# Operand tile of all products laid out by k-tiles with both halves side by side and 32 bytes behind each

## The chip, the cores and the metric

The kernel runs on one core of one Trainium2 chip. The metric is the device time of one execution in microseconds. Three runs of the kernel before gave 1229.66 us as their median (1229.54 to 1230.91 us).

## The reference

Two layers of a decoder trunk work on x of 256 tokens by 2048 channels, all in float32. The first layer is a Mamba-2 mixer: one wide input product, a causal convolution, a scan over one chunk of 256 tokens, a gated norm in 8 groups, and an output product. Its result makes one shared K and V. The second layer is an attention with three groups of heads on that K and V, with a gate and an output product. Every layer ends in a LayerNorm of the residual.

```
h = x * (1 + scale) + shift                 # per layer, from c
proj = h @ a_in_w                           # 2048 -> 10304
y = ssd(conv(xBC), dt) * silu(z), normed    # 256 x 4096
x = LayerNorm(ALPHA*x + (1+gate) * (y @ a_out_w))       # 4096 -> 2048
k, v = split(x @ kv_w)                      # 2048 -> 6144
h = x * (1 + scale1) + shift1
q, z = split(h @ b_in_w)                    # 2048 -> 4096
o = attention(q, k, v) * silu(z)
out = LayerNorm(ALPHA*x + (1+gate1) * (o @ b_out_w))
```

## The kernel before

Nearly all the time goes into the products with the large weights. Every float32 operand of them is split in two float32r tiles, a high half and a low half that holds what the high one lost, and a product is three matmuls: high by high, high by low, low by high. A weight piece of 128x1024 floats is loaded into a tile `raw` (6 buffers, SP's queue), ScalarE copies it to `whi` (line 100) and VectorE writes `raw - whi` to `wlo` (line 102). The other operand, with its 2048 or 4096 channels in k-tiles of 128, stays in one tile, `actT`, that the program takes four times over: as `hp` (the input of layer one, lines 339 and 340), `yp` (the input of the first output product, lines 866 and 867), `xp` (the input of K, V, the queries and the second gate, lines 944 and 945), and at the end as `gl`, which holds rows of gate and norm (line 1218) and feeds no product.

Three helpers write all these matmuls, and they use `actT` in three ways:

- `cm_piece` (lines 151 to 153): weights stationary, 256 columns of `actT` moving, four blocks of 128 output channels for each k-tile, so 12 matmuls of 256 columns for a k-tile.
- `cm_wide` (lines 190 and 193): weights stationary; for the high weights both halves of a k-tile move in one matmul of 512 columns, for the low weights the high half moves alone (256 columns). A k-tile has two of 512, then two of 256. It makes the channels `xs` of groups 2 to 7 from `hp`, and K, the queries and the second gate from `xp`.
- `tm_mults` (lines 224 to 226): the other way round. A block of 128 tokens of `actT` is stationary and 512 columns of weights move; a k-tile has six matmuls. It makes z from `hp`, the first output product from `yp`, V from `xp`, and the second output product from other tiles.

Each matmul has its own weight load, which the profile lists as PEld. The product of `dt` (lines 626 to 628) is of the first kind with 256 moving columns.

Where the bytes lie in a partition matters for what follows. `actT` begins at byte 88320, which is a multiple of 256. The k-tiles of one half of `hp` and of `yp` are 1024 bytes apart and the two halves 16 KB apart; in `xp` a k-tile has its two halves side by side and k-tiles are 2048 bytes apart. `whi` and `wlo` have four buffers each of 4352 bytes, 17 times 256, that begin at multiples of 256 too. `halves_at` shifts what is written in them by an offset that depends on the helper: `SHORT` (16 floats, 64 bytes) for `cm_piece`, `WIDE` (48 floats, 192 bytes) for `cm_wide`, `LONG` (none) for `tm_mults`. So with all distances taken modulo 256 bytes, the weights lie 64 bytes behind the operand in every matmul of `cm_piece`, 192 behind it in every one of `cm_wide`, and at the same place in every one of `tm_mults`, whatever the k-tile and the buffer.

The order of the work is that of the code: each engine runs what the program issues for it in that order, with a few `issue_after` that hold a step behind another.

Of the kernel before, what the change touches and what calls it, by code (L numbers as in the profile page):

```python
# [9 lines left out]
F32 = mybir.dt.float32  # L10
F32R = mybir.dt.float32r
# [7 lines left out]
P = 128  # L19
L = 256  # L20
D = 2048
KT = D // P
# [18 lines left out]
    _o += _s  # L41
NPAR = _o

CI, CT, CM, NCONST = 0, 128, 256, 384

CD, CG, NBIAS = 0, 512, 1024

# [2 lines left out]
def trunk(ctx, tc, xT, x, c, par, cst, bias, lnrow, ada, wdt, win, wxs, wout, wk, wv, wbin, wbout, out):  # L50
# [5 lines left out]
    act = ctx.enter_context(tc.tile_pool(name="act", bufs=1))  # L56
# [15 lines left out]
    cc = cons.tile([P, NCONST], F32, name="cc")  # L72
# [4 lines left out]

    ident = cc[:, CI:CI + 128]
    tri = cc[:, CT:CT + 128]
    ones = cc[:, CM:CM + 128]  # L80
    cons.tile([P, 32], F32, name="pad")
    SHORT, WIDE, LONG = (16, 16), (48, 48), (0, 0)

# [24 lines left out]
    def settle():  # L108

        while owed:  # L110
            with tc.issue_after(copied[-1].ins), tc.issue_after(latest[-1].ins):
                owed.pop(0)()

    def first_or(src, q, off=(0, 0)):

        return ready.pop() if ready else split(load_piece(src[q]), off=off)

    def begin_next():

        if upcoming:  # L120
            src, q, off = upcoming.pop(0)
            ready.append(split(load_piece(src[q]), off=off))

    def behind_next():

        stack = ExitStack()
        if ready:
            stack.enter_context(tc.issue_after(copied[-1].ins))
            stack.enter_context(tc.issue_after(latest[-1].ins))
        return stack  # L130

    def background(n, every=1):

        state[0] += n
        while state[0] >= every and jobs:
            state[0] -= every
            jobs.pop(0)()
# [25 lines left out]
    def acc_pair(pool=None):  # L163
        return [(pool or mm).tile([P, 2, L], F32, name="acc") for _ in range(2)]
# [10 lines left out]

    def cm_wide(src, dst, rate=(0, 1), moving=None, later=False, seen=lambda a: a):

        both, high = moving or (lambda kt: xp[:, kt], lambda kt: xhi[:, kt, :])
        ps = acc_pair()
        for q in range(KT // 4):  # L180
            w = first_or(src, q, WIDE)
            if q == 1:
                settle()
            if q == KT // 4 - 1:
                begin_next()
            hi, lo = (t.rearrange("p k n -> p (k n)").rearrange("p (k n) -> p k n", k=4) for t in w)
            for k in range(4):
                kt = 4 * q + k
                for n in range(2):
                    T.matmul(ps[n], hi[:, k, n * P:n * P + P], both(kt), start=kt == 0, stop=False,  # L190
                             skip_group_check=True)
                for n in range(2):
                    T.matmul(ps[n][:, 0, :], lo[:, k, n * P:n * P + P], high(kt), start=False, stop=kt == KT - 1,  # L193
                             skip_group_check=True)
            background(*rate)
        def put():
            for n in range(2):
                d = dst[:, n, :]
                if seen is by_time:
                    d = d.rearrange("p (b m h) -> p b m h", b=2, h=2)  # L200
                S.activation(d, seen(ps[n][:, 1, :]), AF.Copy)
                V.tensor_tensor(d, seen(ps[n][:, 0, :]), d, op=ALU.add)

        if later:
            owed.append(put)
        else:
            with behind_next():
                put()
# [127 lines left out]
            jobs.pop(0)()  # L336


    hp = act.tile([P, 2, KT, L], F32R, name="actT")
    hhi, hlo = hp[:, 0], hp[:, 1]  # L340


    slots = ctx.enter_context(tc.tile_pool(name="slots", bufs=1))
# [1 line left out]
    with ExitStack() as cA:  # L345
# [15 lines left out]
        with ExitStack() as cS:  # L361
# [38 lines left out]
            def xs_wide(g):  # L400

                xs[g] = pxs.tile([P, 4, L], F32, name="xs")
                for w in range(2):
                    t = xs[g][:, 2 * w:2 * w + 2, :]
                    cm_wide(wxs[2 * g - 4 + w], t, rate=R, moving=(lambda kt: hp[:, :, kt, :], hh_))
                    for n in range(2):
                        conv(t[:, n, :], 4 * g + 2 * w + n, t[:, n, :])

# [31 lines left out]
            with ExitStack() as c0:  # L440
# [83 lines left out]
                for row in ("b4:0. b6:0. h z2:0. z1:0. b2:0 x1:0 h", "b2:1. x1:1. z1:1. z4:0 h h",  # L524
# [3 lines left out]
                    for w in row.split():  # L528
                        if w == two:
                            n = -2 if sum(o[0] == -2 for o in order) == sum(o[0] == -1 for o in order) else -1  # L530
# [160 lines left out]
            R = (1, 10)  # L691
# [171 lines left out]
        aux = ctx.enter_context(tc.tile_pool(name="auxb", bufs=2, space=PSUM, reuse_waits="tile"))  # L863

        pn = cA.enter_context(tc.tile_pool(name="pn", bufs=1, reuse_waits="tile"))
        yp = act.tile([P, 2, KT, L], F32R, name="actT")
        yhi = [yp[:, 0], yp[:, 1]]
        ylo = {g: pn.tile([P, 4, L], F32R, name=f"ylo{g}") for g in (1, 2, 3, 4, 7, 5, 6)}

        def y_ahead(q):  # L870
# [70 lines left out]
                    normalise(b, 256, 512)  # L941


    xp = act.tile([P, KT, 2, L], F32R, name="actT")
    xhi, xlo = xp[:, :, 0, :], xp[:, :, 1, :]
    pb = ctx.enter_context(tc.tile_pool(name="pb", bufs=1))
    hx, lx = (lambda kt: xhi[:, kt, :]), (lambda kt: xlo[:, kt, :])

# [52 lines left out]
    with ExitStack() as cL:  # L1001
# [3 lines left out]
        def high(i, b):  # L1005
            for k in range(2):
                kt = 2 * (i // 2) + k
                for w in first_v[i]:
                    T.matmul(vps[i % 2][b], hx(kt)[:, b * P:b * P + P], w[:, k, :], start=kt == 0 and w is first_v[i][0],  # L1009
                             stop=False)  # L1010
# [6 lines left out]
        end, _ = x_quad(0)  # L1017
# [5 lines left out]
        for i in range(4):  # L1023
            if i == 2:
                _, tile4 = x_quad(1)
# [10 lines left out]
        for q in range(2, KT // 2):  # L1036
# [3 lines left out]
            for j in range(2):  # L1040
                with tc.issue_after(end.ins):
                    w = split(load_piece(wv[2 * j][q]), after=tile4.ins if q == 2 else None)
# [4 lines left out]
        R = (1, 2)  # L1047
# [19 lines left out]
        for kt in range(KT):  # L1067
            t = pl.tile([P, L], F32, name="htmp")
# [10 lines left out]
    R = (0, 1)  # L1079
# [135 lines left out]
        z_gate(hq, qs[hq])  # L1215
    drain()

    gl = act.tile([P, 2, 2, D], F32, name="actT")
    gt, lnt = gl[:, 0], gl[:, 1]
    og = (lambda kt: oghi[kt // 4][:, kt % 4, :]), (lambda kt: oglo[kt // 4][:, kt % 4, :])  # L1220

# [64 lines left out]
    mv0, r0, _ = root(0, lambda mv: None)  # L1286
# [29 lines left out]
    _, r1, step = root(1, between)  # L1316
# [34 lines left out]
def _layout(x, c, ada_w, ada_b, ln_g, ln_b, a_in_w, a_conv_w, a_conv_b, a_dt_bias,  # L1351
            a_A_log, a_D, a_norm_g, a_out_w, kv_w, b_in_w, b_out_w):
    f = np.float32
    crow = np.concatenate([c.reshape(KT, P), np.eye(KT, dtype=f)], 1)
    par = np.zeros((P, NPAR), f)

    def put(name, a):
        par[:a.shape[0], OFF[name][0]:OFF[name][1]] = a

    ab = ada_b.reshape(2, 3, KT, P)  # L1360
    put("adab", ab.transpose(3, 0, 2, 1).reshape(P, 96))
    put("convw", a_conv_w[0].T.reshape(48, P, 4).transpose(1, 0, 2).reshape(P, 192))
    put("convb", _cm(a_conv_b[0]))
    put("normg", _cm(a_norm_g[0]))
    put("dsk", np.broadcast_to(a_D[0], (P, 64)))
    put("dtb", a_dt_bias[0][:, None])
    put("alog", np.broadcast_to(a_A_log[0], (P, 64)))
    put("lng", _cm(ln_g[0]))
    put("lnb", _cm(ln_b[0]))

    cst = np.zeros((P, NCONST), f)
    i = np.arange(P)
    cst[:, CI:CI + 128] = np.eye(P)
    up = (i[:, None] <= i[None, :]).astype(f)
    cst[:, CT:CT + 128] = up
    cst[:, CM:CM + 128] = 1.0
    bias = np.zeros((P, NBIAS), f)
    half, m = i // 64, i % 64
    same = 4 * (m[:, None] - m[None, :]) + 2 * (half[:, None] - half[None, :])
    own = 4 * (m[:, None] - m[None, :])  # L1380
    second = half[:, None] != half[None, :]

    def mask(delta, win_, dil):
        return np.where((delta >= 0) & (delta % dil == 0) & (delta <= win_), 0.0, NEG)

    ratio = np.where(second, SLOPES[2 * H], SLOPES[H]) / SLOPES[0]
    bias[:, CD:CD + 512] = np.concatenate([-same - 1, -same, -own * ratio, 1 - same], 1)
    bias[:, CG:CG + 512] = np.concatenate([mask(same + 1, 128, 1), mask(same, 128, 1),
                                           np.where(second, mask(own, 2048, 16), mask(own, 512, 4)),
                                           mask(same - 1, 128, 1)], 1)  # L1390

    ada = ada_w.reshape(2, D, 3, KT, P).transpose(0, 2, 3, 4, 1)

    w = a_in_w[0]
    z, xs, bb, cc, dt = (w[:, a:b] for a, b in ((0, 4096), (4096, 8192), (8192, 9216), (9216, 10240), (10240, 10304)))
    bc = np.stack([bb.reshape(D, G, P), cc.reshape(D, G, P)], 2).reshape(D, 2048)
    win = _pieces(np.concatenate([bc, xs[:, :1024], z], 1))
    return {
        "xT": x[0].T.reshape(KT, P, L).transpose(1, 0, 2), "x": x[0], "c": np.concatenate([crow, np.zeros_like(crow), crow]), "par": par, "cst": cst, "bias": bias,
        "lnrow": np.stack([ln_g[0], ln_b[0], ln_g[1], ln_b[1]]),  # L1400
        "ada": ada, "wdt": _dt(dt), "win": win, "wxs": _pieces(xs[:, 1024:], 256, 4),
        "wout": _pieces(a_out_w[0]), "wk": _pieces(kv_w[:, :3072], 256, 4),
        "wv": _pieces(kv_w[:, 3072:]), "wbin": _pieces(b_in_w[0], 256, 4), "wbout": _pieces(b_out_w[0]),
    }
# [20 lines left out]
```

## Time and profile before

| | |
|---|---|
| median of 3 runs | 1229.66 us |
| the profiled execution | 1229.02 us |
| its span | 1227.2 us |
| PE busy | 1212.2 us |
| VectorE busy | 1018.8 us |
| ScalarE busy | 705.4 us |
| HBM traffic | 273 GB/s mean over the span |
| granted TensorE clock | 1.0 |

The profile is of one execution. PE is TensorE's matmuls and PEld its weight loads; DVE is VectorE, ACT is ScalarE. The matmuls overlap each other in the records: the duration of one is longer than the distance to the next one's start, so the pace of a stream is read from the starts, in the timeline, and not from the durations. The timeline merges equal instructions that follow each other into one row with their count.

### The profile page before, as it was taken

To read this page: it belongs to the slowest core of one execution; us is meant where nothing else is said; L and a number is where in the kernel's file an instruction comes from. 1 tells how busy PE (TensorE), PEld (TensorE's weight loads), DVE (VectorE), ACT (ScalarE), POOL (GpSimd) and SP (SyncE) were. 2 spreads that over 40 slices of the span, in tenths; PEclk is the share of its full clock that TensorE was granted. 3 is DMA by queue.
4 is the path that set the end of the run, shared out by engine and by line. 5 is a ranking of instruction groups with operands and counts; after the bars stand their busy time and mean duration, and the time that the engine had idled before them with its cause. 6 is when DMAs were issued, how large, how long until landed. Compare 5 with 4: busy or idle time off the path is not lost.

```text
span 1227.2 us, 19063 instructions
## 1 busy us (share of the span) xinstructions
PE 1212.2 (99%) x7244; PEld 1038.8 (85%) x7244; DVE 1018.8 (83%) x1448; ACT 705.4 (57%) x1058; POOL 3.9 (0%) x8
## 2 busy tenths in 40 slices
PE   8899999999999999999999999999999999999998
PEld 7789988898888888888888788888887888888886
DVE  6999996999988989899778578888987875756786
ACT  3555577878597789754335455444435744444751
POOL 0000000000000000000000000000000000000001
PEclk9999999999999999999999999999999999999999
DMA  9999977686666556599988669989997775365673
GB/s 372 422 421 422 422 269 243 224 304 242 226 207 205 170 168 213 188 343 337 382 298 309 217 190 350 346 343 382 383 380 277 262 275 173 112 191 162 193 258 69
DMA packets 81372, 335.94 MB, mean 274 GB/s; under 512 B 9200, under 2 KB 9984, under 8 KB 68480
## 3 DMA queue, kind: packets, MB, share of 16 engines
q1 hardware_dynamic: 80352, 333.33, 74.6%
q0 software_dynamic: 576, 1.05, 0.6%
q8 instruction: 57, 0.93, 0.3%
q10 hardware_dynamic: 352, 0.34, 0.1%
q14 instruction: 35, 0.29, 0.1%
HBM read 331.45 MB, written 3.23 MB: 273 GB/s over the span
## 4 chain that ended last, share of the span: by engine, by line
PE 81%; DMA 8%; DVE 6%; ACT 3%; issue 2%; DVEq 0%; ACTq 0%; SPq 0%
PE acc L190 24%; PE acc L193 12%; PE acc L225 11%; PE acc L226 11%; PE acc L224 11%; DMA raw<-in_win 6%; DVE wlo L102 2%; DVE araw L306 2%; PE py L787 1%; ACT whi L100 1%; PE acc L151 1%; PE acc L153 1%; DMA araw<-in_ada 1%; PE acc L152 1%; PE acc L1009 1%
## 5 line engine op out<-in xcount | busy, mean ns | idle before, releaser
L100 ACT ACTIVATE whi<-raw 128x1024 fp32r<-128x1024 f32 x389 | 408.0, 1057 | 355.8 <-PE acc L226 126.0
L102 DVE TENSOR_TENSOR wlo<-raw,whi 128x1024 fp32r<-128x1024 f32 x389 | 468.9, 1221 | 140.2 <-ACT whi L100 138.7
L190 PE MATMUL acc<-actT,whi 128*128 128x512 f32 x1280 | 401.1, 394 | 0.0
L193 PEld LDWEIGHTS acc<-actT,wlo 128*128 128x128 f32 x1280 | 239.5, 188 | 52.6 <-DVE wlo L102 0.3
L225 PE MATMUL acc<-wlo,actT 128*128 128x512 f32 x656 | 257.5, 392 | 3.3 <-DVE wlo L102 3.3
L193 PE MATMUL acc<-actT,wlo 128*128 128x256 f32 x1280 | 254.7, 280 | 0.0
L224 PE MATMUL acc<-whi,actT 128*128 128x512 f32 x656 | 253.6, 394 | 0.2 <-ACT whi L100 0.2
L306 DVE SCALAR_TENSOR_TENSOR araw<-araw,cb__72 128x2048 f32<-128x2048 f32 x95 | 217.0, 2284 | 3.4 <-DMA araw<-in_ada 3.1
L190 PEld LDWEIGHTS acc<-actT,whi 128*128 128x128 f32 x1280 | 194.7, 188 | 0.8
L226 PE MATMUL acc<-whi,actT 128*128 128x512 f32 x432 | 168.8, 391 | 0.0
L225 PEld LDWEIGHTS acc<-wlo,actT 128*128 128x128 f32 x656 | 123.2, 188 | 31.0 <-DVE wlo L102 6.0
L224 PEld LDWEIGHTS acc<-whi,actT 128*128 128x128 f32 x656 | 122.5, 188 | 24.7 <-ACT whi L100 0.6
L151 PE MATMUL acc<-actT,whi 128*128 128x256 f32 x372 | 103.0, 281 | 2.5 <-ACT s L646 1.4
L153 PE MATMUL acc<-actT,wlo 128*128 128x256 f32 x372 | 101.8, 282 | 1.4 <-DVE wlo L102 1.1
L152 PE MATMUL acc<-actT,whi 128*128 128x256 f32 x372 | 102.9, 279 | 0.0
L226 PEld LDWEIGHTS acc<-whi,actT 128*128 128x128 f32 x432 | 81.1, 188 | 16.7
L226 PE MATMUL acc<-whi,ylo 128*128 128x512 f32 x224 | 87.6, 391 | 0.0
L151 PEld LDWEIGHTS acc<-actT,whi 128*128 128x128 f32 x372 | 69.7, 188 | 3.7 <-ACT s L646 1.8
L153 PEld LDWEIGHTS acc<-actT,wlo 128*128 128x128 f32 x372 | 68.8, 188 | 2.5 <-DVE wlo L102 2.3
L152 PEld LDWEIGHTS acc<-actT,whi 128*128 128x128 f32 x372 | 70.5, 190 | 0.2
L226 PEld LDWEIGHTS acc<-whi,ylo 128*128 128x128 f32 x224 | 42.1, 188 | 8.6
L745 ACT ACTIVATE seg<-cbc,cumT 128x128 f32<-128x128 f32 x128 | 41.1, 389 | 2.2 <-PE py L787 2.1
(313 smaller groups left out, 1125.5 us busy)
## 6 DMA issues: line engine op xcount, KB each, us to landing
araw<-in_ada SPq DMA_DIRECT2D x96, 1024.0 KB, 7.5
raw<-in_win SPq DMA_DIRECT2D x109, 512.0 KB, 6.3
raw<-in_wout SPq DMA_DIRECT2D x64, 512.0 KB, 5.8
raw<-in_wbin SPq DMA_DIRECT2D x64, 512.0 KB, 3.7
raw<-in_wxs SPq DMA_DIRECT2D x48, 512.0 KB, 4.5
raw<-in_wv SPq DMA_DIRECT2D x48, 512.0 KB, 6.3
raw<-in_wk SPq DMA_DIRECT2D x48, 512.0 KB, 7.3
cbc<-cumd SPq DMA_DIRECT2D x16, 512.0 KB, 5.0
```

What stands on the lines that cost most here:

```text
L100: copied.append(S.activation(hi, raw, AF.Copy))
L102: latest.append(V.tensor_tensor(lo, raw, hi.bitcast(F32), op=ALU.subtract))
L151: T.matmul(o, hi[:, k, c_], ahi[:, kt, :], start=first, stop=False, skip_group_check=True)
L152: T.matmul(o, hi[:, k, c_], alo[:, kt, :], start=False, stop=False, skip_group_check=True)
L153: T.matmul(o, lo[:, k, c_], ahi[:, kt, :], start=False, stop=kt == k1 - 1, skip_group_check=True)
L190: T.matmul(ps[n], hi[:, k, n * P:n * P + P], both(kt), start=kt == 0, stop=False, skip_group_check=True)
L193: T.matmul(ps[n][:, 0, :], lo[:, k, n * P:n * P + P], high(kt), start=False, stop=kt == KT - 1, skip_group_check=True)
L224: T.matmul(o, h_, hi[:, k, :], start=kt == k0, stop=False, skip_group_check=part)
L225: T.matmul(o, h_, lo[:, k, :], start=False, stop=False, skip_group_check=part)
L226: end = T.matmul(o, l_, hi[:, k, :], start=False, stop=kt == k1 - 1, skip_group_check=part)
L306: return V.scalar_tensor_tensor(raw, raw, 1.0, cb_, op0=ALU.mult, op1=ALU.mult, accum_out=mod[layer][:, ct, j:j + 1])
L745: S.activation(seg[:, hh, b, :], cbc[:, hh, b, :], AF.Relu, bias=cumT[:, b, h0 + hh:h0 + hh + 1], scale=-1.0)
```

## The change

The tile `actT` gets one shape for all uses: 16 k-tiles of 520 floats, that is, 256 of the high half, 256 of the low half, and 8 that are not used (32 bytes). A helper `operand` takes it and gives the whole, the high halves and the low halves. With `hp` the matmul of 512 columns now reads one run of 512 floats and not two runs of 256; with `xp` nothing but the padding is new; with `yp` the two operands `yhi[0]` (k-tiles 0 to 15) and `yhi[1]` (16 to 31) now lie side by side k-tile by k-tile. k-tiles are 2080 bytes apart, so from each to the next the address modulo 256 goes on by 32 bytes.

The tile is 512 bytes longer. They come from the tile of constants: its block of ones goes, and the one matmul that used it reads a column of the triangle `tri`, which is all ones, with a step of 0. The load of the constants is 128x256 floats and no longer 128x384. In the partition, `actT` begins at byte 87808 and no longer 88320, `raw`, `whi` and `wlo` lie 512 bytes lower, and what comes behind `actT` stays where it was. On every engine the program has the same instructions in the same order as before, with the same waits.

```diff
-CI, CT, CM, NCONST = 0, 128, 256, 384
+CI, CT, NCONST = 0, 128, 256
...
-    ones = cc[:, CM:CM + 128]
+    ones = tri[:, 127:128].to_broadcast([P, P])
...
-        both, high = moving or (lambda kt: xp[:, kt], lambda kt: xhi[:, kt, :])
+        both, high = moving or (lambda kt: xp[:, kt, 0:2 * L], lambda kt: xhi[:, kt, :])
...
-    hp = act.tile([P, 2, KT, L], F32R, name="actT")
-    hhi, hlo = hp[:, 0], hp[:, 1]
+    ROW = 2 * L + 8
+
+    def operand():
+
+        t = act.tile([P, KT * ROW], F32R, name="actT").rearrange("p (k n) -> p k n", n=ROW)
+        return t, t[:, :, 0:L], t[:, :, L:2 * L]
+
+    hp, hhi, hlo = operand()
...
-                    cm_wide(wxs[2 * g - 4 + w], t, rate=R, moving=(lambda kt: hp[:, :, kt, :], hh_))
+                    cm_wide(wxs[2 * g - 4 + w], t, rate=R, moving=(lambda kt: hp[:, kt, 0:2 * L], hh_))
...
-        yp = act.tile([P, 2, KT, L], F32R, name="actT")
-        yhi = [yp[:, 0], yp[:, 1]]
+        _, *yhi = operand()
...
-    xp = act.tile([P, KT, 2, L], F32R, name="actT")
-    xhi, xlo = xp[:, :, 0, :], xp[:, :, 1, :]
+    xp, xhi, xlo = operand()
...
-    gl = act.tile([P, 2, 2, D], F32, name="actT")
+    gl = act.tile([P, KT * ROW], F32, name="actT")[:, :4 * D].rearrange("p (i j n) -> p i j n", i=2, j=2)
```

More of the change, by code (lines that the diff above doesn't have):

```diff
@@ L1375, in _layout @@
     cst[:, CT:CT + 128] = up
-    cst[:, CM:CM + 128] = 1.0
     bias = np.zeros((P, NBIAS), f)
```

## Prediction

> **What bounds the kernel now.** I read the page first, for the engine that sets the span.
>
> ```profile
> span 1227.2 us, 19063 instructions
> PE 1212.2 (99%) x7244; PEld 1038.8 (85%) x7244; DVE 1018.8 (83%) x1448; ACT 705.4 (57%) x1058; POOL 3.9 (0%) x8
> ...
> PE 81%; DMA 8%; DVE 6%; ACT 3%; issue 2%; DVEq 0%; ACTq 0%; SPq 0%
> PE acc L190 24%; PE acc L193 12%; PE acc L225 11%; PE acc L226 11%; PE acc L224 11%; DMA raw<-in_win 6%; DVE wlo L102 2%; DVE araw L306 2%; PE py L787 1%; ACT whi L100 1%; PE acc L151 1%; PE acc L153 1%; DMA araw<-in_ada 1%; PE acc L152 1%; PE acc L1009 1%
> ```
>
> The chain that ended last is four fifths TensorE, most of it the matmuls of the two helpers `cm_wide` (L190, L193) and `tm_mults` (L224 to L226). The change removes no work and moves none; if it does anything, it changes the pace of matmuls. So the next view is the groups of instructions, for the counts.
>
> ```profile
> L190 PE MATMUL acc<-actT,whi 128*128 128x512 f32 x1280 | 401.1, 394 | 0.0
> L193 PE MATMUL acc<-actT,wlo 128*128 128x256 f32 x1280 | 254.7, 280 | 0.0
> L224 PE MATMUL acc<-whi,actT 128*128 128x512 f32 x656 | 253.6, 394 | 0.2 <-ACT whi L100 0.2
> L225 PE MATMUL acc<-wlo,actT 128*128 128x512 f32 x656 | 257.5, 392 | 3.3 <-DVE wlo L102 3.3
> L226 PE MATMUL acc<-whi,actT 128*128 128x512 f32 x432 | 168.8, 391 | 0.0
> L151 PE MATMUL acc<-actT,whi 128*128 128x256 f32 x372 | 103.0, 281 | 2.5 <-ACT s L646 1.4 <-ACT actT L513 1.1
> ```
>
> `cm_wide` has 1280 / 2 = 640 k-tiles, `tm_mults` 1744 matmuls (328 k-tiles) with `actT` stationary, `cm_piece` 372 / 4 = 93 k-tiles of 12. The third view is the timeline, read by starts. First `tm_mults` and the `dt` product, each undisturbed.
>
> ```profile
> 640.06 0.39 PE L224 MATMUL acc<-whi,actT 128*128 128x512 f32 x1
> ...
> 641.42 0.39 PE L224 MATMUL acc<-whi,actT 128*128 128x512 f32 x1
> ```
>
> ```profile
> 165.77 0.28 PE L626 MATMUL acc<-actT,whi 128*128 128x256 f32 x1
> ...
> 167.13 0.28 PE L626 MATMUL acc<-actT,whi 128*128 128x256 f32 x1
> ```
>
> Six matmuls of 512 columns in 1.36 us are 226.7 ns each; twelve of 256 in 1.36 us are 113.3 ns. No long stretch goes faster, so I call these the floor. A k-tile of `cm_wide` would be 2 x 226.7 + 2 x 113.3 = 680 ns at it. This is what it takes, first with `xp` (K), then with `hp` (xs).
>
> ```profile
> 820.41 0.62 PE L190 MATMUL acc<-actT,whi 128*128 128x512 f32 x2
> 820.86 0.40 PE L193 MATMUL acc<-actT,wlo 128*128 128x256 f32 x2
> 821.10 0.62 PE L190 MATMUL acc<-actT,whi 128*128 128x512 f32 x2
> 821.56 0.39 PE L193 MATMUL acc<-actT,wlo 128*128 128x256 f32 x2
> 821.79 0.62 PE L190 MATMUL acc<-actT,whi 128*128 128x512 f32 x2
> ```
>
> ```profile
> 268.25 0.62 PE L190 MATMUL acc<-actT,whi 128*128 128x512 f32 x2
> ...
> 269.63 0.62 PE L190 MATMUL acc<-actT,whi 128*128 128x512 f32 x2
> ```
>
> Two k-tiles take 1.38 us in both, 690 ns each: 10 ns over the floor, with no wait in between, over and over in the same two-k-tile pattern. And `cm_piece` has two paces, at the same distance modulo 256 between its operands:
>
> ```profile
> 205.73 0.28 PE L151 MATMUL acc<-actT,whi 128*128 128x256 f32 x1
> ...
> 207.14 0.28 PE L151 MATMUL acc<-actT,whi 128*128 128x256 f32 x1
> ```
>
> ```profile
> 245.63 0.28 PE L151 MATMUL acc<-actT,whi 128*128 128x256 f32 x1
> ...
> 246.31 0.28 PE L151 MATMUL acc<-actT,whi 128*128 128x256 f32 x1
> ```
>
> Twelve in 1.41 us (117.5 ns) in one product, six in 0.68 us (113.3 ns) in another. Where a matmul of 256 columns has its operands at the same place modulo 256, in the last product, it goes slowest:
>
> ```profile
> 1212.23 0.28 PE L226 MATMUL acc<-bs,s 128*128 128x256 f32 x1
> ...
> 1213.43 0.28 PE L224 MATMUL acc<-whi,s 128*128 128x256 f32 x1
> ```
>
> Ten in 1.20 us, 120 ns each. So a stream keeps one of two paces until something disturbs it, and the longer one differs between distances 0 and 64 (120 and 117.5 ns). That is the opening for the change: now all k-tiles of a product repeat one distance, afterwards eight distances follow each other.
>
> **The change part by part.**
>
> One run of 512 instead of two of 256 in the products with `hp`: nothing. The two `cm_wide` fences above are this very comparison, 16 KB apart and side by side, and both show 1.38 us for two k-tiles.
>
> The other readers and writers of `actT`, ScalarE and VectorE, get other strides:
>
> ```profile
> L515 DVE TENSOR_TENSOR actT<-htmp,actT 128x256 fp32r<-128x256 f32 x16 | 6.8, 424 | 0.1
> ...
> L254 DVE TENSOR_TENSOR actT<-htmp,actT 128x256 fp32r<-128x256 f32 x16 | 6.2, 419 | 0.0
> ```
>
> The same subtraction into `hp` and into `xp`, 424 and 419 ns: layout has at most 16 x 5 ns in it. Nothing. The ones read by step 0 are the weights of one float32 matmul (L713), and the constants' load is a third shorter; both stand once and off the chain's named lines. Nothing, with some tenths of a microsecond either way.
>
> `cm_wide`, 640 k-tiles, 10 ns over the floor each: 6.4 us that a change of distance can reach. From above the end is the floor, -6.4 us. From below, the nearest row is the pace of the last product, 120 - 113.3 = 6.7 ns on each matmul of 256, now paid for about half of them; 640 x 6.7 = +4.3 us. I take half the gain, -3.2 us: of eight distances some must lie as badly as those now in use, and the only two for which this trace has 256-column streams both have a pace above the floor, but a pattern that needs the same distance every time cannot go on through all of them.
>
> `cm_piece`, 93 k-tiles, at most 1.41 - 1.36 = 0.05 us each: 4.7 us if all went at 117.5 ns, and some already are at the floor. Ends -4.7 and, all at 120 ns, 93 x 12 x (120 - 117.5) = +2.8 us. I take a third of the gain, -1.6 us, since much of it lies where TensorE waits:
>
> ```profile
> 70.00:240.00 170.00, 168.48 (x1149) 152.25 (x1148) 150.85 (x200) 109.99 (x161) 0.00 (x0) 1.00 0.86 330
> ...
> 760.00:925.00 165.00, 165.00 (x913) 143.41 (x912) 140.46 (x143) 72.66 (x92) 0.00 (x0) 1.00 0.94 369
> ```
>
> The table by stretches (length, then busy time of PE, PEld, DVE, ACT, POOL, then clock, DMA share and GB/s) shows VectorE at 150.85 of 170 us there, and some of a faster matmul is lost to the next `wlo`. In the stretch of K, 760 to 925, nothing but TensorE is full, and DMA at 369 GB/s would have to go 690/680 faster, 374 GB/s, under the 422 of the page's best slice:
>
> ```profile
> GB/s 372 422 421 422 422 269 243 224 304 242 226 207 205 170 168 213 188 343 337 382 298 309 217 190 350 346 343 382 383 380 277 262 275 173 112 191 162 193 258 69
> ```
>
> `tm_mults`, 1744 matmuls: already at the floor with a constant distance of 0, so here the change can only lose. What a stream pays to find its floor again is seen after a wait:
>
> ```profile
> 1182.94 0.40 PE L225 MATMUL acc<-wlo,s 128*128 128x512 f32 x1
> ...
> 1185.25 0.39 PE L226 MATMUL acc<-whi,s 128*128 128x512 f32 x1
> ```
>
> Ten matmuls in 2.31 us and not in 2.267: 43 ns in all, 4.3 ns each, and then 226.7 ns again. The lower end is 0 (the floor does not mind 32 bytes), the upper a stream that never settles, 1744 x 4.3 = +7.5 us. Between them, a step of 32 bytes is 8 of 512 columns, 226.7 / 64 = 3.5 ns of the stream; if each k-tile's step is made up by one such delay, that is 328 x 3.5 = 1.1 us. I take +1.1 us, nearer to 0, because a stream at the floor is seen to stay there across all changes of buffer, half and block.
>
> Sum: -3.2 - 1.6 + 1.1 = -3.7 us. The profiled execution took 1229.02 us (1.8 around its span); 1229.0 - 3.7 = 1225.3. The median of the runs lies 0.64 us higher, so 1226.0 us.
>
> **The rivals.**
>
> *Nothing happens.* The excess belongs to the order 512, 512, 256, 256 and to how a stream was started, not to addresses. For it: `cm_piece` goes at 113.3 and at 117.5 ns at one distance. Against it: 120 ns at distance 0, a pace that neither `cm_piece` nor `dt` has. Time: 1229.7 us. The Trainium skill speaks for this rival: "TensorE: Matmul & The Clock Gate", section "Part 2: What happens when you issue a matmul", says that moving operand and weight load have read ports of their own and that a load takes no bandwidth from the running matmul. By that rule no distance matters and the sum is 0; the trace does not refute it, but the 120 ns above have no explanation in it.
>
> *Slower: streams never settle.* Each k-tile gets a new distance after 4 to 12 matmuls, and a stream needs about ten to settle (43 ns, above). `tm_mults` then loses its floor, +7.5 us, and `cm_wide` and `cm_piece` only change one pattern for another, 0: 1229.7 + 7.5 = 1237.2 us. For it: `tm_mults` is the largest stage at the floor, and its distance of 0 is the only one at which a 512-column stream is seen there. Against it: the floor holds through jumps of 256 bytes and more. It decides as soon as more than 4.8 / 7.5 = two thirds of the k-tiles restart the search, since the forecast's gain is 4.8 us.
>
> *The whole gain.* Every such pattern goes and no floor is lost: 1229.7 - 6.4 - 3.3 (`cm_piece` with some of it at the floor already) = 1220.0 us.
>
> **How the numbers follow.** Forecast, about half the excess gone: 0.35. The whole gain, or most of it: 0.09. Nothing happens: 0.22. Slower by lost floors: 0.34. A difference of about 0.2% (2.5 us) is what a measurement of this kernel can tell from none. Faster: 0.35 + 0.09 = 0.44; within: 0.22; slower: 0.34. Two signs hold most of the chance. The likeliest case's own range is 1222 to 1228 us; the range to hold the time 8 times in 10 goes from the whole gain to the slower rival, 1220 to 1237 us.
>
> **What would show it.** In the profile afterwards, `cm_wide` should take less than 690 ns for a k-tile and no longer repeat one pattern of two; eight k-tiles should make a period, since 8 x 32 = 256. `cm_piece` should be below 1.41 us for a k-tile from the start, and `tm_mults` should show 1.36 us for six in most places, with small delays once for each k-tile at most. With two k-tiles of `cm_wide` still at 1.38 us, the rival that nothing happens is right; with `tm_mults` above 1.37 us for six through whole products, the slower one. If waits of TensorE for `wlo` or for pieces grow by as much as the pace gains, the pace was read rightly and its worth was not.

## The result and the profile after

The changed kernel took 1242.53 us (median of 4 runs, 1242.0 to 1243.73), the kernel before beside it 1229.6 us (1228.94 to 1230.91). The ratio is 1.0111, with an interval of 1.0098 to 1.0123: slower by 12.9 us, where 3.7 us of gain were forecast. The profiled execution took 1242.76 us. One of the ten runs of e1 below took 4288.15 us and is left out of its median; all other times are of undisturbed runs.

The page after, its first rows and the head of its chain:

```profile
span 1240.9 us, 19063 instructions
PE 1228.6 (99%) x7244; PEld 1044.8 (84%) x7244; DVE 1019.8 (82%) x1448; ACT 707.2 (57%) x1058; POOL 3.9 (0%) x8
...
PE 93%; DMA 3%; DVE 2%; ACT 1%; issue 1%; DVEq 0%; ACTq 0%
```

The counts are the same, VectorE and ScalarE have grown by 1.0 and 1.8 us, PE by 16.4, and TensorE's share of the chain has gone from 81% to 93%, as it would if slower matmuls filled waits of before. The groups of instructions:

```profile
L190 PE MATMUL acc<-actT,whi 128*128 128x512 f32 x1280 | 404.0, 396 | 0.0
L193 PE MATMUL acc<-actT,wlo 128*128 128x256 f32 x1280 | 257.0, 282 | 0.0
L224 PE MATMUL acc<-whi,actT 128*128 128x512 f32 x656 | 256.5, 398 | 0.1
L225 PE MATMUL acc<-wlo,actT 128*128 128x512 f32 x656 | 260.2, 397 | 2.5 <-DVE wlo L102 2.5
L226 PE MATMUL acc<-whi,actT 128*128 128x512 f32 x432 | 170.8, 395 | 0.0
```

Every group is up by 2 to 3 us, the matmuls of `tm_mults` (L224, L225) from 394 and 392 ns to 398 and 397. The pace itself is read from the starts in the timeline. `cm_wide` with `xp` (K), the stretch that took 690 ns for a k-tile:

```profile
858.24 0.62 PE L190 MATMUL acc<-actT,whi 128*128 128x512 f32 x2
...
858.93 0.63 PE L190 MATMUL acc<-actT,whi 128*128 128x512 f32 x2
...
859.63 0.62 PE L190 MATMUL acc<-actT,whi 128*128 128x512 f32 x2
...
863.84 0.62 PE L190 MATMUL acc<-actT,whi 128*128 128x512 f32 x2
```

The last of these rows begins eight k-tiles after the first: 5.60 us, 700 ns each, and from there the same eight follow again. The pattern of two is gone and the period is eight, as foreseen, but at 20 ns over the floor and not under 10. `tm_mults` in the first output product:

```profile
639.68 0.39 PE L224 MATMUL acc<-whi,actT 128*128 128x512 f32 x1
...
645.25 0.39 PE L224 MATMUL acc<-whi,actT 128*128 128x512 f32 x1
```

These are 24 matmuls apart: 5.57 us, 232.1 ns each, where it ran at its floor of 226.7. The product of `dt`, which had run at 113.3 ns, and a product of `cm_piece` that had:

```profile
165.16 0.28 PE L632 MATMUL acc<-actT,whi 128*128 128x256 f32 x1
...
166.59 0.28 PE L632 MATMUL acc<-actT,whi 128*128 128x256 f32 x1
```

```profile
249.95 0.28 PE L151 MATMUL acc<-actT,whi 128*128 128x256 f32 x1
...
251.73 0.28 PE L151 MATMUL acc<-actT,whi 128*128 128x256 f32 x1
```

Twelve in 1.43 us are 119.2 ns, and fifteen in 1.78 us are 118.7. No stream of the changed kernel that reads `actT` is left at the floor.

The whole loss can be laid out from the trace: for every float32r matmul, the time from its start to the next one's less its floor, added up, without the steps that are over 15 ns longer, which are waits.

| over the floor, us (ns each) | before | after |
|---|---|---|
| `cm_piece` | 3.3 (2.97) | 5.3 (4.85) |
| `cm_wide`, 512 columns | 3.2 (2.58) | 6.6 (5.24) |
| `cm_wide`, 256 columns | 3.5 (2.80) | 6.4 (5.04) |
| `tm_mults` and the 48 like matmuls of V's first pieces, `actT` stationary | 1.8 (1.04) | 9.6 (5.57) |
| `tm_mults`, `ylo` stationary | 0.2 | 1.4 |
| `dt` | 0 | 0.25 |

That is 17.5 us more; the span has grown by 13.7, so some 3.8 us must lie where TensorE waited anyway. One place where they do is the input product before the scan. The one float32 matmul that reads the ones stands behind it; this is its own line's view, before and then after (count, shortest, median and longest in ns, first and last start in us):

```profile
L713 PE MATMUL aux<-araw,cc x2: 222/248/275, 195.7 to 195.8; 128*128 128x64 f32 x2
```

```profile
L719 PE MATMUL aux<-araw,cc x2: 222/248/275, 195.8 to 195.8; 128*128 128x64 f32 x2
```

It begins at the same time to 0.1 us and takes the same 222 and 275 ns: nothing has been lost up to there, and reading the ones with a step of 0 costs nothing. Behind it the loss builds up where TensorE alone sets the pace. In the stretch of K (length, then busy time and count of PE, PEld, DVE, ACT, POOL, then clock, DMA share and GB/s):

```profile
760.00:925.00 165.00, 165.00 (x901) 142.24 (x901) 141.51 (x146) 72.16 (x90) 0.00 (x0) 1.00 0.94 363
```

901 matmuls stand where 913 stood, with the clock at 1.00 in both.

### The profile page after: what moved, and what is told of

It reads as the page before. It is cut to its first block, busy times and chain, and to the rows that moved or that the text cites. A ratio compares the mean times of both kernels' runs of the same rounds, so it can differ in the third digit from the quotient of the medians.

```text
span 1240.9 us, 19063 instructions
## 1 busy us (share of the span) xinstructions
PE 1228.6 (99%) x7244; PEld 1044.8 (84%) x7244; DVE 1019.8 (82%) x1448; ACT 707.2 (57%) x1058; POOL 3.9 (0%) x8
## 4 chain that ended last, share of the span: by engine, by line
PE 93%; DMA 3%; DVE 2%; ACT 1%; issue 1%; DVEq 0%; ACTq 0%
PE acc L190 24%; PE acc L225 13%; PE acc L226 13%; PE acc L224 13%; PE acc L193 12%; PE acc L151 3%; PE acc L153 3%; PE acc L152 3%; DMA raw<-in_win 3%; PE py L793 1%; DVE wlo L102 1%; PE acc L1013 1%; PE po L1164 1%; PE aux L846 1%; DMA adab<-in_par 1%; PE aux L784 1%
## 5 line engine op out<-in xcount | busy, mean ns | idle before, releaser
L225 PE MATMUL acc<-wlo,actT 128*128 128x512 f32 x656 | 260.2, 397 | 2.5 <-DVE wlo L102 2.5
L224 PE MATMUL acc<-whi,actT 128*128 128x512 f32 x656 | 256.5, 398 | 0.1
L226 PE MATMUL acc<-whi,actT 128*128 128x512 f32 x432 | 170.8, 395 | 0.0
L225 PEld LDWEIGHTS acc<-wlo,actT 128*128 128x128 f32 x656 | 123.3, 188 | 33.0 <-DVE wlo L102 5.1
L224 PEld LDWEIGHTS acc<-whi,actT 128*128 128x128 f32 x656 | 122.6, 188 | 27.2 <-ACT whi L100 0.5
```

Source lines behind the costliest of these rows:

```text
L224: T.matmul(o, h_, hi[:, k, :], start=kt == k0, stop=False, skip_group_check=part)
L225: T.matmul(o, h_, lo[:, k, :], start=False, stop=False, skip_group_check=part)
L226: end = T.matmul(o, l_, hi[:, k, :], start=False, stop=kt == k1 - 1, skip_group_check=part)
```

## The experiments

Two theories were left. **Price of distance**: each distance, modulo 256 bytes, between the operand's address and that of the weights has a pace of its own for each helper, and the three offsets of before were picked where it is low. **Price of change**: a stream pays whenever the distance changes, as the slower rival of the prediction had it, and a constant distance would be free. In the first eight runs `actT` keeps its 33,280 bytes, so that nothing behind it moves. All of them change only these lines of the changed kernel, with S = 0, 8, 16, ... 56 floats in `operand` (where the line below has S, the run has its number):

```diff
-    ROW = 2 * L + 8
+    ROW, SIZE = 2 * L, KT * (2 * L + 8)
...
-        t = act.tile([P, KT * ROW], F32R, name="actT").rearrange("p (k n) -> p k n", n=ROW)
+        t = act.tile([P, SIZE], F32R, name="actT")[:, S:S + KT * ROW].rearrange("p (k n) -> p k n", n=ROW)
...
-    gl = act.tile([P, KT * ROW], F32, name="actT")[:, :4 * D].rearrange("p (i j n) -> p i j n", i=2, j=2)
+    gl = act.tile([P, SIZE], F32, name="actT")[:, :4 * D].rearrange("p (i j n) -> p i j n", i=2, j=2)
```

**e1**, S = 0: the layout by k-tiles without the padding.

> The changed kernel without its 32 bytes behind each k-tile: k-tiles 2048 bytes apart, halves side by side, ones and addresses as changed, so one distance modulo 256 for each helper as before. If the padding (the distance that changes with each k-tile) is what cost 13 us, this takes what the kernel before took, 1229.6 us within 2.5, with 690 ns for a k-tile of cm_wide and 1.36 us for six matmuls of tm_mults. If the halves side by side in hp and yp, the shift of whi and wlo by 512 bytes or the ones read by step 0 cost something, it stays above 1233.

**e2** to **e4**, S = 8, 16, 24: one constant distance, 32, 64 and 96 bytes further than before.

> As e1, but the whole operand tile begins 32 bytes later, so the distance is another one (by 32) but still the same for all k-tiles. If what costs is the change from k-tile to k-tile (no stream settles), this is within 4 us of 1229.6 and every helper shows a short repeated pattern, tm_mults at or near 226.7 ns a matmul. If certain distances cost by themselves, those that are no multiple of 64 bytes first of all, it shows the price here in full: tm_mults at 230 ns or more throughout, about +6 us from it alone, 1236 or more in all.

> As e2 with 64 bytes: distance 64 for tm_mults, 128 for cm_wide (operand behind weights), 0 for cm_piece. By the price of change: within 4 us of 1229.6, with cm_piece slower than before (120 ns a matmul as the last product has at distance 0: up to +3 us of 1116 matmuls). By the price of a distance: tm_mults above its floor, since it now has the distance at which cm_piece ran at 117.5.

> As e2 with 96 bytes. By the price of change: within 4 us of 1229.6. By the price of a distance: near e2 if what counts is being off a multiple of 64, between e1 and e2 if the price falls with distance.

**e5** to **e8**, S = 32, 40, 48, 56, complete the circle.

> Operand tile 128 bytes later, one distance for all k-tiles. If each distance has its own price and a change of distance costs nothing beside, the mean of the eight shifts (0 to 224) is the changed kernel, 13 us over the one before: the first four gave 0, 18, 15 and 17 us, so the remaining four must give 13 x 8 - 50 = 54 us together, 13 to 14 each, and by helper their means over the eight shifts must be those of the changed kernel: 5.6 ns a matmul over the floor for tm_mults, 4.9 for cm_piece, 5.0 and 5.2 for the 256 and 512 columns of cm_wide. If change costs beside, that sum comes out clearly lower, under 35 us.

> As e5, with 160 bytes. By the price of each distance: 8 to 20 us over the kernel before, part of the sum of 54 us; tm_mults above its floor everywhere. With change as the price: under 9 us.

> As e5, with 192 bytes. cm_wide then has distance 0 (256 behind 256), where the last product's matmuls of 256 columns took 120 ns each: its 256-column matmuls at 5 to 7 ns over the floor; its 512-column ones nearer to their floor, if what tm_mults shows at 0 holds for them. tm_mults itself as at 64 on the other side, 5 to 7 ns. 10 to 18 us over the kernel before; with change as the price, under 9 us.

> As e5, with 224 bytes, 32 to the other side of the kernel before. If only the nearness to the distances of before counts, this is the cheapest of the seven shifts, under 8 us; by the price of each distance with no order that is known yet, 10 to 18 us.

Measured (us, the kernel before on the same chip beside it; the four columns on the right are ns over the floor for each matmul, as in the table above):

| run | us | before | ratio, interval | `cm_piece` | wide 512 | wide 256 | `tm_mults` |
|---|---|---|---|---|---|---|---|
| e1, 0 | 1228.72 | 1228.60 | 1.0000, 0.9991 to 1.0010 | 2.49 | 2.56 | 2.83 | 1.04 |
| e2, 32 | 1246.83 | 1228.60 | 1.0147, 1.0131 to 1.0162 | 4.95 | 5.80 | 7.16 | 6.04 |
| e3, 64 | 1243.67 | 1228.60 | 1.0118, 1.0101 to 1.0135 | 6.52 | 4.54 | 4.10 | 6.45 |
| e4, 96 | 1245.36 | 1228.60 | 1.0136, 1.0121 to 1.0151 | 3.44 | 7.01 | 4.63 | 6.39 |
| e5, 128 | 1239.91 | 1229.22 | 1.0086, 1.0071 to 1.0101 | 3.19 | 4.22 | 2.68 | 5.90 |
| e6, 160 | 1246.19 | 1229.22 | 1.0139, 1.0124 to 1.0154 | 6.58 | 6.16 | 5.15 | 6.21 |
| e7, 192 | 1236.59 | 1229.22 | 1.0059, 1.0042 to 1.0076 | 5.40 | 6.49 | 2.12 | 3.26 |
| e8, 224 | 1240.85 | 1229.22 | 1.0095, 1.0080 to 1.0110 | 4.37 | 2.00 | 5.28 | 6.85 |
| mean of the eight | | | | 4.62 | 4.85 | 4.24 | 5.27 |
| changed kernel | 1242.53 | 1229.60 | 1.0111, 1.0098 to 1.0123 | 4.85 | 5.24 | 5.04 | 5.57 |

e1 has all of the change but the 32 bytes, and takes the time of before. The timeline of K in it shows the old pace, 1.38 us for two k-tiles:

```profile
820.53 0.62 PE L190 MATMUL acc<-actT,whi 128*128 128x512 f32 x2
...
821.91 0.62 PE L190 MATMUL acc<-actT,whi 128*128 128x512 f32 x2
```

e2 has a distance that never changes, and loses more than the changed kernel. The timelines of K and of the first output product in it:

```profile
835.60 0.63 PE L190 MATMUL acc<-actT,whi 128*128 128x512 f32 x2
...
836.30 0.63 PE L190 MATMUL acc<-actT,whi 128*128 128x512 f32 x2
...
837.72 0.63 PE L190 MATMUL acc<-actT,whi 128*128 128x512 f32 x2
```

```profile
651.90 0.39 PE L224 MATMUL acc<-whi,actT 128*128 128x512 f32 x1
...
653.99 0.39 PE L224 MATMUL acc<-whi,actT 128*128 128x512 f32 x1
```

Three k-tiles take 2.12 us, 707 ns each, and nine matmuls of `tm_mults` 2.09 us, 232.2 ns each, again and again in one rhythm. A stream that meets the same distance every time is slow for ever. Price of change, as the whole of the loss, falls here. e3 puts `cm_piece` at distance 0, the one at which the last product had run at 120 ns:

```profile
205.01 0.28 PE L151 MATMUL acc<-actT,whi 128*128 128x256 f32 x1
...
206.81 0.28 PE L151 MATMUL acc<-actT,whi 128*128 128x256 f32 x1
```

Fifteen in 1.80 us are 120.0 ns, as that row of the prediction had it. The eight runs add up to 96.8 us over the kernel before, 12.1 on the mean, and the changed kernel, which goes through all eight distances, loses 12.9. The last four give 46.7 us together, where the sum had asked for 54 and a price of change alone for less than 35. Group by group the excess of the changed kernel is that of the mean plus 0.2 to 0.8 ns.

K-tile by k-tile the account is less exact. These are the k-tiles of `cm_wide`, ns over the floor for a whole one, means without those that hold a wait:

| shift of the k-tile, bytes | 0 | 32 | 64 | 96 | 128 | 160 | 192 | 224 |
|---|---|---|---|---|---|---|---|---|
| changed kernel | 12.9 | 24.1 | 22.7 | 21.4 | 23.5 | 19.3 | 19.9 | 19.3 |
| e1 to e8, that shift in all k-tiles | 10.6 | 26.0 | 17.1 | 23.4 | 13.7 | 22.7 | 17.0 | 14.4 |

A k-tile shifted by 128 bytes costs 23.5 ns among k-tiles with other shifts and 13.7 among its like. So the sum fits, but a k-tile doesn't simply pay the price of its own distance; what its neighbours have counts as well.

Of the guesses within the distances several missed: for e7 I had the 256-column matmuls of `cm_wide` at 5 to 7 ns and its 512-column ones near the floor, and it is 2.12 and 6.49; its 7.4 us are under the 10 to 18 expected. e8 was to be the cheapest of the seven shifts, under 8 us, if nearness to the old distance counted, and costs 11.6 us. A small distance from the old one is no guide.

Could it be the other engines, which write and read the weights meanwhile, or the DMA? The traces say no. In e2 the 11 k-tiles of `cm_wide` in which VectorE and ScalarE both ran for less than a tenth of the time are 26.6 ns over the floor, and the 216 in which both ran for more than nine tenths 25.1. The 38 k-tiles with the DMA engines at most 2% busy are at 25.6 ns, the 316 with over 90% at 26.1.

**e9** moves operand and weights together. Operand and weights of layer one's input product and of everything with `xp` go up by 32 bytes; with `yp` and in the last product both stay. Left out below are the lines that set `base` and `by` back to 0 there, and those of `ROW`, `SIZE` and `gl`, which are as in e1:

```diff
+    base = [8]
...
-        return [wp.tile([P, 1088], F32R, name=n, bufs=4)[:, o:o + 1024] for n, o in zip(("whi", "wlo"), off)]
+        return [wp.tile([P, 1088], F32R, name=n, bufs=4)[:, o + base[0]:o + base[0] + 1024] for n, o in zip(("whi", "wlo"), off)]
...
+    def operand(by=8):
...
+        t = act.tile([P, SIZE], F32R, name="actT")[:, by:by + KT * ROW].rearrange("p (k n) -> p k n", n=ROW)
```

> As e2 the operand tile begins 32 bytes later (for hp and xp; yp stays), but whi and wlo are written 32 bytes further on as well in the products with hp and xp, so that every distance modulo 256 is that of the kernel before (but for 48 matmuls of the first V pieces) while the addresses themselves are off a multiple of 64. If the price belongs to the distance between operand and weights, this takes 1229 us within 2.5, and cm_wide 690 ns for a k-tile. If it belongs to an address that is no multiple of 64 bytes, or to a collision of the operand with something else than the weights, cm_wide and cm_piece stay at the excess of e2 (16 us against 7 for cm_wide, 5.5 against 3 for cm_piece), 1240 us or more.

1229.46 us beside 1229.04, ratio 1.0002 (0.9993 to 1.0012). The timeline of K in e9:

```profile
820.37 0.62 PE L192 MATMUL acc<-actT,whi 128*128 128x512 f32 x2
...
821.75 0.62 PE L192 MATMUL acc<-actT,whi 128*128 128x512 f32 x2
```

1.38 us for two k-tiles once more. In e2 the same move of the operand alone cost 18.2 us; it is the distance that counts and not the operand's own address. And in e2 to e8 all loads of weights lie among themselves as they did in e1, and so do all moving operands, in every product that reads `actT` alone; only the distance from the ones to the others is new. So it is between these two that the time is lost there.

**e10** and **e11** ask whether a distance between those of 32 bytes is better. They are the kernel before with its offsets for `cm_piece` and `cm_wide` 16 bytes up and 16 bytes down:

```diff
-    SHORT, WIDE, LONG = (16, 16), (48, 48), (0, 0)
+    SHORT, WIDE, LONG = (20, 20), (52, 52), (0, 0)    # e10
+    SHORT, WIDE, LONG = (12, 12), (44, 44), (0, 0)    # e11
```

> The kernel before with the weights of cm_wide and cm_piece 16 bytes further behind the operand (WIDE 52 floats, SHORT 20; LONG stays). A step half as large as any so far. If the price goes smoothly with the distance, cm_wide moves part of the way from 7 us over the floor to the 9 us of e8, and the time stays within 3 us of before; if 16 bytes are enough to leave the good place, it costs as much as the 32-byte shifts did in cm_wide and cm_piece, 3 to 12 us. A faster kernel is possible only if a place between the 32-byte ones is better: cm_wide and cm_piece together have 10 us over the floor.

> As e10 to the other side (WIDE 44 floats, SHORT 12): if smooth, between before and e2, up to 6 us slower; if 16 bytes are enough to leave the good place, 3 to 12 us slower.

1235.58 and 1235.53 us beside 1229.04, ratios 1.0055 (1.0040 to 1.0070) and 1.0057 (1.0042 to 1.0072). `cm_piece` goes to 5.32 and 4.89 ns over its floor, `cm_wide` to 5.75 and 7.32 for its matmuls of 512 columns, while `tm_mults`, whose offset stays, keeps 1.03 and 1.07. So 16 bytes are enough to lose 6.5 us, and no version better than the kernel before came out of this.

**e12** asks whose distance it is: that to the weights a matmul uses, or that to the weights loaded meanwhile for the next one. It is the kernel before with `wlo` alone 32 bytes lower:

```diff
-    SHORT, WIDE, LONG = (16, 16), (48, 48), (0, 0)
+    SHORT, WIDE, LONG = (16, 8), (48, 40), (0, 0)
```

> The kernel before with wlo alone 32 bytes lower (SHORT (16, 8), WIDE (48, 40)), so that only the distance of the operand to wlo becomes that of the operand shifted by 32 bytes; whi keeps its own. In a k-tile of cm_wide the four matmuls are over their floors by 1.2, 3.9, 3.3, 2.3 ns in the kernel before and by 6.3, 5.2, 4.0, 10.4 ns with the operand shifted by 32 bytes (e2; means over 608 and 610 k-tiles). Theory that the distance to the weights in use sets the pace: the last two, which use wlo, go as in e2 (4.0 and 10.4) and the first two as before (1.2 and 3.9): 8.8 ns a k-tile, 5.6 us over 640, and with a third of cm_piece's matmuls some 6 us in all, 1235. Theory that the distance to the weights loaded meanwhile does: during the second and third matmul wlo is loaded, so they go as in e2 (5.2 and 4.0), the first and last as before (1.2 and 2.3): 2.0 ns a k-tile, 1.3 us, in all 1230 to 1231. Neither, if the pattern of a k-tile comes out with the first and the last both changed: then the four matmuls are one rhythm and no single distance sets a matmul's pace. tm_mults with actT has whi and wlo at offset 0 and does not change.

1239.21 us beside 1229.27, ratio 1.0083 (1.0069 to 1.0096): more than either theory gave. The four matmuls of a k-tile of `cm_wide`, ns over the floor:

| | 1st, `whi` | 2nd, `whi` | 3rd, `wlo` | 4th, `wlo` | sum |
|---|---|---|---|---|---|
| before | 1.2 | 3.9 | 3.3 | 2.3 | 10.7 |
| e2, operand + 32 | 6.3 | 5.2 | 4.0 | 10.4 | 25.9 |
| e12, `wlo` - 32 | 5.3 | 12.5 | 5.2 | 3.6 | 26.6 |

The timeline of K in e12 shows it too:

```profile
840.10 0.63 PE L190 MATMUL acc<-actT,whi 128*128 128x512 f32 x2
...
840.81 0.63 PE L190 MATMUL acc<-actT,whi 128*128 128x512 f32 x2
...
842.92 0.63 PE L190 MATMUL acc<-actT,whi 128*128 128x512 f32 x2
```

Four k-tiles in 2.82 us, 705 ns each. The two matmuls with `whi`, whose own distance hasn't moved, lose 4.1 and 8.6 ns; those with `wlo`, whose distance has, 1.9 and 1.3. So a matmul's pace is not set by the distance to its own weights alone. The most is lost in the second, in which `wlo` is loaded, which is where the other theory put its loss; but it is 8.6 ns and not 1.3, and the first matmul has changed too. That is the third outcome named above: the four matmuls and their loads are one rhythm. Here `whi` and `wlo` also lie 32 bytes from each other, which they do in no other run; that this has a price of its own isn't excluded.

The first eight runs show the same without that doubt. In the first output product the third matmul of each group has `ylo` stationary and `whi` moving, and neither of the two moves in e1 to e8; only its neighbours read `actT`. It runs 1.1 ns over the floor in the kernel before, 1.0 in e1, and 1.6 to 7.7 in e2 to e8.

## Why the prediction was wrong

**`tm_mults`, +1.1 us: the largest miss.** The step that failed was "I take +1.1 us, nearer to 0, because a stream at the floor is seen to stay there across all changes of buffer, half and block". All those changes are multiples of 256 bytes: the distance stayed 0, and the trace of before held no case of `tm_mults` with `actT` at another one. Measured are 7.8 us with `actT` stationary and 1.2 us with `ylo`; e2 to e8 give 3.3 to 6.9 ns for each matmul at any of the other seven distances, where 0 has 1.04. The range for the term (0 to +7.5) ends 0.3 short of the first of the two, and had nothing for `ylo`.

**`cm_wide`, -3.2 us.** The failed step was to take half the gain since "of eight distances some must lie as badly as those now in use". The sample that I argued from, 64, 192 and 0, was where the kernel's offsets had put each helper, and for `cm_wide` and `tm_mults` these are the best of the eight. Over a whole k-tile of `cm_wide`, that is two of each kind, no other shift is below 2 x (2.56 + 2.83) = 10.8 ns; the nearest, e5, has 13.8. For `cm_piece` a shift of 128 is as good as none: 3.19 ns in e5, and 2.49 to 3.25 in the kernel before, e1 and e9, which all have the old distance. Measured for `cm_wide` is +6.2 us. The lower bound, +4.3, was too small as well: it charged only the matmuls of 256 columns, and those of 512 have lost 3.4 of the 6.2. I had looked for what was above the floor and took it for what a change could win; that the other distances are worse was only a bound in the sum, and it is what the runs show. The second ground, that the only two distances with streams of 256 columns lie above the floor, misread the trace of before: `cm_wide` has such streams at a third distance, 192, and at 64 a part of `cm_piece` is at the floor.

**`cm_piece`, -1.6 us.** Measured +2.1, inside the ends (-4.7 to +2.8). The row of 120 ns at distance 0 was the one that told the price of that distance, and e3 shows that price in `cm_piece` itself.

**The slower rival, 1237.2 us.** Its side was right, and its 7.5 us for `tm_mults` is near the 7.8 measured, but its mechanism is refuted: e2 never changes its distance and is slower than the changed kernel. That the two figures lie so close is luck. By that mechanism `cm_wide` and `cm_piece` lost nothing, and so its time and with it the top of my range came out 5 us too low.

**The rule that speaks for no effect.** In e2 and e12 the same matmuls and loads run at other distances, and the kernel takes 1.0147 and 1.0083 times as long. The Trainium skill, "TensorE: Matmul & The Clock Gate", section "Part 2: What happens when you issue a matmul", gives operand and weight load read ports of their own, and a load that takes no bandwidth from the running matmul. By that rule, as the prediction read it, no distance matters and both ratios would be 1; the runs disagree.

**What was right.** Both halves side by side, the 512 bytes by which `actT` and the pieces move, and the ones read with a step of 0 cost nothing (e1: 1.0000, and the L719 row). The period of eight k-tiles came. Nothing but TensorE is full in the stretch of K, and some of what the matmuls lose is hidden in front of the scan; both were read from the table by stretches.

**What stays open.** The changed kernel lies 0.8 us above the mean of the eight distances, less than its interval of 1.5 us to either side; a small price of the change itself may be in it, and wasn't isolated; the table by k-tiles shows that neighbours matter. Why some distances are slow isn't known. In e2 to e8 the moving operand meets a load of weights, but e12 doesn't tell whether consecutive loads can also hold each other up. And `cm_piece` has two paces at one distance: in the kernel before and in e1 its k-tiles take 113.3 or 117.8 ns for each matmul, and the pace changes only behind a wait of TensorE or behind another product. The k-tiles from 121 to 131 us go at 117.8 ns in the one and at 113.3 in the other. So there the pace hangs on how the stream was started, as the rival that nothing happens had it for the whole excess; what picks it isn't known.

## What to carry to other kernels

Where streams of matmuls follow each other without a wait, give operand and weights one fixed distance modulo 256 bytes and find it by measuring: there are only eight on a grid of 32 bytes (e10 and e11 show that 16 bytes matter too), and going through all of them cost about the mean here, not the best. A quantity that a trace shows at one value only, however often, says nothing about its other values; before trusting a floor across "all changes", ask whether the thing about to change ever changed. And what a stream runs above its floor is no reserve as long as it isn't shown that any other setting gets it.

## What the runs showed of the hardware

- The pace of a stream depends on the distance of its two operands modulo 256 bytes: for 512 columns in `tm_mults` 227.7 ns on the mean at distance 0 against 229.9 to 233.5 at the other seven (1.04 against 3.26 to 6.85 over the floor of 226.7), for 256 columns 113.3 to 120.0 ns. Over this kernel it is up to 1.0147 in time, at a granted clock of 1.0.
- Moving both by the same 32 bytes changes nothing (e9, 1.0002), and neither do steps of 256: the four buffers of `whi` are 17 times 256 bytes apart, and in the kernel before the k-tiles of K are 7 and 13 ns over the floor by turns across all of them.
- A matmul whose own two operands have not moved is slowed by its neighbours' (`ylo`, 1.0 ns over the floor in e1, 6.3 in e2).
- A stream of 256 columns can hold either of two paces at one distance, 113.3 and 117.8 ns, and changes between them only behind a wait or another product (`cm_piece`, the kernel before and e1).
- 16 bytes are a distance of their own (e10 and e11, +6.5 us each). The Trainium skill, "SBUF — State Buffer", section "Specifications (TRN2)", gives cachelines of 16 bytes and a penalty for each new line that is crossed to. All addresses here are multiples of 16, so that rule tells none of these runs apart, and they lie up to 18 us apart.
- Low and high weights on different offsets slow the matmuls of the one that did not move (e12, 12.5 ns over the floor and not 3.9).
